# A one-core mixture-of-experts layer: the first expert pair's rows by a one-hot matmul, and the output stored from ScalarE's queue

## The chip, the cores and the metric

The kernel runs on one core of a Trainium2 chip. A core has TensorE (PE, with its weight load as PEld), VectorE (DVE), ScalarE (ACT), GpSimd (POOL) and SyncE (SP). Each works through its own row of instructions and waits at semaphores for the others. DMAs are issued from an engine's queue (SPq, ACTq, POOLq) and carried out by sixteen DMA engines. The metric is the device time in microseconds of one execution, and the times given are those of several runs.

## The reference

A decoder layer on 512 tokens of 1024 features. The front end (stick-breaking attention beside spatial gating, one input and one output projection) gives h. A router then picks one group of experts and two experts in it for each token:

```python
hn = rmsnorm(h, ffn_norm_g)
h  = h + hierarchical_moe(hn, ...)   # 4 groups of 8 experts, top 1 group, top 2 experts
out = rmsnorm(h, final_norm_g)
# one expert: silu(hn @ w_gate) * (hn @ w_up), times its weight, @ w_down; F = 512
```

All 32 experts have weights of their own: three matrices of 1024 x 512 in fp32, 201 MB in all.

## The kernel before, in words

The tokens lie in four chunks (c = 0 to 3) of 128 partitions, and h stays in SBUF. After the attention, the output projection is worked in eight units u (chunk and half), each followed at a distance by the router's steps. A string of letters for each unit sets their order: o and O are the projection's matmuls, A adds them to h, q squares, t transposes h (`turn`), l gives the logits `lg`, r and R go on with `route` (the small VectorE operations that end in `oab`, the two one-hot choices of each token), m and p give the position of each token in its expert's list (`pos_mm` on TensorE, `positions` on VectorE), M gathers the lists in PSUM (`rows_mm`). The last string, u = 8, is the tail after the last projection. Behind it comes chunk 3 by itself, in the order of the code.

`store_xn(c)` writes the normalized rows of a chunk to the DRAM tensor xn_d. Its ScalarE copy puts feature 8p+k at place (k, p), so that a row of 1024 splits into eight blocks of 128. The gate and up weights are loaded in the order that goes with it.

The experts work in 16 pairs (p = 0 to 15), 64 slots for each expert, so that a pair has 128 rows. `gather(xg, GI[:, p])` is an indirect DMA from GpSimd's queue that fetches the pair's 128 rows of xn_d; GI is made from the lists (`stl` and `gi` in the trace). `prep` transposes the rows in eight blocks on TensorE (`px`) and scales by the norm's gain into XS[p] (`xs`): four blocks on ScalarE, four in one VectorE operation. Then gate and up (`gu`, 32 matmuls for each expert), the activation (`sg`, `gg`, `hg`), down (`y`), the split of y in `yh` and `yl`, and the one-hot matmuls that add the rows back into h (`cb`, at the end `cl`). `busy(pool, tag, n)` makes TensorE work on products that nobody reads (`idle` in the trace). After the lists, VectorE works out counts (`cnt`, `tot`, `cop`, `okt`). The count `n_over` of rows that find no slot is read by four engines into a register (`values_load`, a TENSOR_LOAD), and `If` blocks on such counts jump over the overflow's work, which has nothing to do with these inputs except for the few rows of `xgo`.

The weights come in 192 loads of 1 MiB from SyncE's queue (`load_next`, L592 and L590) into 19 half slots that are freed by the matmuls which read them. The loads stand in SyncE's row in a fixed order, each with a wait for its slot. One small DMA stands among them: `mark_d` takes 16 numbers of the first gather's result to DRAM, and what follows it in SyncE's row comes after it.

The tail: for the last pair `down`, `results` (which makes `yh` and `yl`), then `unit(c, n)` adds half n of chunk c into h, `squares` and `scale_3` make the final norm's factor (GpSimd raises to the power), `gained` and `finish` multiply by gain and factor into fin, and `finish` stores the chunk from SyncE's queue (L1254). Last there is an `If(n_over > OVER)`, L1338, which all engines jump over.

## Time and profile before

| what | value |
|---|---|
| median of 3 runs | 750.05 us (746.28 to 752.68) |
| the profiled execution | 752.61 us |
| its span in the trace | 750.6 us |
| mean granted clock of TensorE | 0.966 |
| PE, DVE, ACT, POOL busy | 706.2, 303.8, 230.1, 81.0 us |
| DMA | 231.03 MB, 308 GB/s over the span |

The span runs from the first to the last instruction that the profiler saw; 2.0 us of the execution lie around it. A queue has a q behind its engine's name. PEclk is the clock that TensorE was granted, as a share of 2.4 GHz, and DMA share is how busy the sixteen DMA engines were in a window.

### The profile page before, as it was taken

The numbers are of one execution on the slowest core, as the hardware profiler recorded it, in microseconds if no ns is written. First come the engines' busy times: TensorE is split into PE (matmuls) and PEld (weight loads), VectorE is DVE, ScalarE is ACT, GpSimd is POOL, SyncE is SP. The second block draws the span as 40 slices with busy tenths as digits, with TensorE's granted clock in tenths as the row PEclk, the third lists the DMA queues.
The fourth block names the chain that finished last, engine by engine and source line by source line (L and its number), as shares of the span: only waits on it lengthen the run. The fifth ranks groups of instructions, "written<-read, shape, count | busy, mean of one in ns | idle before, by whom it ended". The sixth has DMA issues, their size and how long they took to land. (4 is left out here: it accounts for less than half of the span.)

```text
span 750.6 us, 9187 instructions
## 1 busy us (share of the span) xinstructions
PE 706.2 (94%) x3426; PEld 400.1 (53%) x3426; DVE 303.8 (40%) x540; ACT 230.1 (31%) x383; POOL 81.0 (11%) x77
## 2 busy tenths in 40 slices
PE   8999999999999799999999998999999999899992
PEld 7776767678788646444443443334344444344431
DVE  5547558375575712313422403033043133042345
ACT  5564568546345512111211211111111111121124
POOL 0322132114121201000000000000000000000001
PEclk9989699899999899999999999999999999999998
DMA  8802010206629789799999999999999999999953
GB/s 269 347 8 105 1 56 29 84 1 222 241 97 415 269 339 412 303 419 420 417 420 420 417 421 419 420 420 419 419 419 420 417 420 418 421 415 420 406 210 117
DMA packets 42392, 231.03 MB, mean 308 GB/s; under 512 B 6354, under 2 KB 8018, under 8 KB 18258
## 3 DMA queue, kind: packets, MB, share of 16 engines
q1 hardware_dynamic: 39394, 223.81, 73.7%
q0 software_dynamic: 2352, 4.20, 1.6%
q10 hardware_dynamic: 576, 2.10, 0.7%
q8 instruction: 43, 0.70, 0.4%
q14 instruction: 27, 0.22, 0.1%
HBM read 230.22 MB, written 4.19 MB: 312 GB/s over the span
## 5 line engine op out<-in xcount | busy, mean ns | idle before, releaser
L981 PE MATMUL gu<-r,xs 128*64 128x512 f32 x1024 | 229.5, 598 | 9.0 <-DMA r<-w_up 4.7
L981 PEld LDWEIGHTS gu<-r,xs 128*64 128x64 f32 x1024 | 86.2, 138 | 149.9 <-issue 131.6
L1011 PE MATMUL y<-r,hg 128*64 128x512 f32 x512 | 114.3, 596 | 0.0
L993 DVE TENSOR_TENSOR hg<-ft,gg 128x256 f32<-128x256 f32 x32 | 13.4, 420 | 228.5 <-ACT gg L991 221.4
L987 ACT COPY sg<-gu 128x512 f32<-128x512 f32 x32 | 18.7, 586 | 225.0 <-PE gu L981 225.0
L1045 DVE TENSOR_TENSOR h<-cb,h 128x512 f32<-128x512 f32 x120 | 74.2, 681 | 0.0
L1011 PEld LDWEIGHTS y<-r,hg 128*64 128x64 f32 x512 | 35.9, 136 | 66.3 <-issue 51.3
L914 POOL DMA_INDIRECT xg<-xn_d,gi x16 | 16.5, 1028 | 379.1 <-PE px L962 371.6
L1032 DVE SCALAR_TENSOR_TENSOR yl<-y,tab,yh 128x512 fp32r<-128x512 f32 x32 | 23.8, 750 | 66.8 <-ACT yh L1031 65.4
L1039 PE MATMUL cb<-yh,oh 128*128 128x512 f32 x120 | 49.9, 416 | 0.0
L1039 PE MATMUL cb<-yl,oh 128*128 128x512 f32 x120 | 47.3, 394 | 0.0
L1031 ACT ACTIVATE yh<-y,tab 128x512 fp32r<-128x512 f32 x32 | 21.8, 687 | 75.5 <-PE y L1011 74.6
L116 PE MATMUL pT<-xhi,hl_w 128*128 128x512 f32 x80 | 35.2, 440 | 0.0
L117 PE MATMUL pT<-xlo,hl_w 128*128 128x512 f32 x80 | 33.8, 423 | 0.0
L118 PE MATMUL pT<-xhi,hl_w 128*128 128x512 f32 x80 | 33.7, 421 | 0.0
L111 POOL TENSOR_TENSOR hl_w<-wqk,hl_w 128x1024 fp32r<-128x1024 f32 x10 | 24.3, 2434 | 69.5 <-ACT hl_w L110 67.2
L965 ACT ACTIVATE xs<-px,ffk 128x128 f32<-128x128 f32 x64 | 18.2, 368 | 32.5 <-PE px L962 32.5
L116 PE MATMUL pR<-hl_w,xhi 128*128 128x512 f32 x64 | 26.4, 413 | 0.0
L117 PE MATMUL pR<-hl_w,xhi 128*128 128x512 f32 x64 | 26.1, 407 | 0.0
L118 PE MATMUL pR<-hl_w,xlo 128*128 128x512 f32 x64 | 25.9, 405 | 0.0
L999 PEld LDWEIGHTS ft<-identf,sg 128*128 128x128 f32 x128 | 14.6, 140 | 21.1 <-issue 16.1
L1039 PEld LDWEIGHTS cb<-yh,oh 128*128 128x128 f32 x120 | 22.6, 188 | 4.5 <-DVE h L1045 0.2
(262 smaller groups left out, 939.0 us busy)
## 6 DMA issues: line engine op xcount, KB each, us to landing
r<-w_gate SPq DMA_DIRECT2D x64, 1024.0 KB, 19.9
r<-w_up SPq DMA_DIRECT2D x64, 1024.0 KB, 19.9
r<-w_down SPq DMA_DIRECT2D x64, 1024.0 KB, 20.3
wqk<-w_inT SPq DMA_DIRECT2D x10, 512.0 KB, 4.5
wr<-w_inR SPq DMA_DIRECT2D x8, 512.0 KB, 7.3
wo<-w_out SPq DMA_DIRECT2D x8, 512.0 KB, 4.6
xt<-xT SPq DMA_DIRECT2D x8, 256.0 KB, 5.3
h<-xr SPq DMA_DIRECT2D x4, 512.0 KB, 10.0
```

The costliest lines, as they stand in the source:

```text
L111: (nc.gpsimd if pool else nc.vector).tensor_tensor(lo, src, hi.bitcast(F32), op=OP.subtract)
L116: nc.tensor.matmul(ps, lh, rh, start=first, stop=False)
L117: nc.tensor.matmul(ps, lh, rl, start=False, stop=False)
L118: nc.tensor.matmul(ps, ll, rh, start=False, stop=last)
L965: nc.scalar.activation(xs[:, k], px[:, k, :xs.shape[2]], AF.Copy, scale=ffk[:, k:k + 1])
L981: nc.tensor.matmul(ps[rs_], xs[:, k], w, start=k == 0, stop=k == KD - 1, skip_group_check=True)
L987: nc.scalar.copy(SG[e], GU[e].rearrange("s (p j) -> s j p", j=4))
L1011: nc.tensor.matmul(YS[p][n][rs_], HT[e][:, j], down_weights(e, j, n), start=j == 0, stop=j == 3, skip_group_check=True)
L1031: nc.scalar.activation(yh[:, cs], YS[p][n], AF.Copy, scale=tab[:, 1, p:p + 1])
L1032: nc.vector.scalar_tensor_tensor(yl[:, cs], YS[p][n], tab[:, 1, p:p + 1], yh[:, cs].bitcast(F32), op0=OP.mult, op1=OP.subtract)
L1039: nc.tensor.matmul(ps, OHT[p][:, c * P:(c + 1) * P], y[:, n * 512:(n + 1) * 512], start=first and i == 0, stop=last and i == 1, skip_group ...
L1045: nc.vector.tensor_tensor(h[:, c, cs], ps, h[:, c, cs], op=OP.add)
```

## The change

The first pair's rows no longer go through DRAM. `first_slots(c)` makes a one-hot `own` for each chunk on VectorE (128 tokens by 128 slots, with the token's norm factor as its value): two operations for q, the slot numbers of the tokens that chose expert 0 or 1, and two comparisons with `slot1`. `first_rows(c, ...)` multiplies h by it on TensorE, eight 128x128 fp32 products for each chunk, summed over the chunks in the PSUM tiles pf0 and pf1. They hold what the transposes held before, and `with_gain` scales them into XS[0]. The letters S and V place `first_slots`, 1 and 2 place `first_rows` for chunk 0; chunks 1 and 2 come after `store_xn(3)`, chunk 3 after its `pos_mm` and `first_slots`. The gather of pair 1 is now the first gather, and stands where that of pair 0 stood. mark_d, all the `busy` calls shown and the load of a second gain vector go. `positions(1)` moves from u = 8 to u = 7. xn keeps the natural order of the features, and the host lays the gate and up weights out to suit; bytes and shapes of the loads stay.

In the tail, the last pair's down for its second half is done in one piece, ahead of the units, with `results(1)` right behind it and `places` after `results(0)`. The four stores are issued by ScalarE, and SyncE has nothing left ahead of the last branch.

The diff, with hunks of little content left out:

```diff
     "o s r R q t m p O A w l M a",
-    "o r R q t m p O A w l M a",
+    "o r R q t m p O A w l M S a",
     "o s r R q t m p O A w l M a",
-    "z q t m k p l M",
+    "z q 1 t 2 m k S p V l M",
 )
...
     xn_d = dram.tile([T, D], F32, name="xn_d")
-    mark_d = dram.tile([1, 16], F32, name="mark_d")
...
     dma(wrs, wr)
-    ffgs = rw.tile([P, KD], F32, name="ffgs")
-    dma(ffgs, ffg)
     brB = rw.tile([P, 36], F32, name="brB")
...
     ffk = keep.tile([P, KD], F32, name="ffk")
-    dma(ffk, ffp)
+    dma(ffk, ffg)
     load_next(2)
...
-        xn[c] = rw.tile([P, KD, P], F32, tag="xn", bufs=2, name=f"xn{c}")
-        nc.scalar.activation(xn[c], h[:, c].rearrange("t (p k) -> t k p", k=KD), AF.Copy, scale=rs2[:, c:c + 1])
+        xn[c] = rw.tile([P, D], F32, tag="xn", bufs=2, name=f"xn{c}")
+        nc.scalar.activation(xn[c], h[:, c], AF.Copy, scale=rs2[:, c:c + 1])
         nc.scalar.dma_start(xn_d[c * P:(c + 1) * P], xn[c])
+    own = rw.tile([P, NCH, P], F32, name="own")
+    slot1 = rw.tile([P, SLOTS], F32, name="slot1")
+    nc.gpsimd.iota(slot1, pattern=[[1, SLOTS]], base=1, channel_multiplier=0, allow_small_or_imprecise_dtypes=True)
+    px0 = []
+    def first_slots(c):
+        q = rw.tile([P, 2, 2], F32, tag="q", bufs=2, name=f"q{c}")
+        nc.vector.tensor_tensor(q[:, 0], oab[:, 0, c, :2], oab[:, 1, c, :2], op=OP.add)
+        nc.vector.scalar_tensor_tensor(q[:, 1], pos_ps[:, c * 32:c * 32 + 2], 1.0, q[:, 0], op0=OP.add, op1=OP.mult)
+        for r, rs_ in halves:
+            nc.vector.tensor_scalar(own[:, c, rs_], slot1, q[:, 1, r:r + 1], rs2[:, c:c + 1], op0=OP.is_equal,
+                                    op1=OP.mult)
+    def first_rows(c, *ks):
+        if not px0:
+            px0.extend(op_.tile([P, 4, P], F32, tag="o", name=f"pf{n}") for n in range(2))
+        for kk in ks:
+            nc.tensor.matmul(px0[kk // 4][:, kk % 4], h[:, c, kk * P:(kk + 1) * P], own[:, c],
+                             start=c == 0 and kk % 4 == 0, stop=c == NCH - 1 and kk % 4 == 3, skip_group_check=True)
...
             pos_mm(2 if u == 8 else (u - 5) // 2)
-        elif x == "p" and u in (5, 8):
-            for k in (0,) if u == 5 else (1, 2):
-                positions(k)
+        elif x == "p" and u in (5, 7, 8):
+            positions({5: 0, 7: 1, 8: 2}[u])
+        elif x in "SV":
+            first_slots({"S": u - 7 + (u == 6), "V": 2}[x])
+        elif x in "12":
+            first_rows(0, *((0, 1, 2) if x == "1" else (3, 4, 5, 6)))
         elif x == "w" and u == 0:
             for k in range(KD):
-                nc.vector.tensor_scalar(wrs[:, k], wrs[:, k], ffgs[:, k:k + 1], None, op0=OP.mult)
+                nc.vector.tensor_scalar(wrs[:, k], wrs[:, k], ffk[:, k:k + 1], None, op0=OP.mult)
         elif x == "l" and u > 0:
...
     store_xn(3)
+    first_rows(0, 7)
+    for c in (1, 2):
+        first_rows(c, *range(KD))
     go(16, R[3])
...
     nc.scalar.activation(ge, gd, AF.Exp)
-    busy(op_, "o", 2)
     nc.scalar.activation(rr, dd, AF.Exp)
-    busy(op_, "o", 2)
     nc.scalar.preload_act_table_set("silu_and_others")
     pos_mm(3)
+    first_slots(3)
     positions(3)
+    first_rows(3, *range(KD))
     rows_mm(sps, soh, (3,))
...
-    gather(xg, GI[:, :1])
-    dma(mark_d, xg[:1, :16])
+    gather(xg, GI[:, 1:2])
     load_next(1)
...
-    wp.close()
-    attp.close()
     rws.close()
...
     nc.gpsimd.memset(xgo, 0.0)
+    XS, GU, SG, HT, YS, YT, OHT = {}, {}, {}, {}, {}, {}, {}
+    def with_gain(xs, px, n):
+        if n == 0:
+            for k in range(4):
+                nc.scalar.activation(xs[:, k], px[:, k, :xs.shape[2]], AF.Copy, scale=ffk[:, k:k + 1])
+        else:
+            nc.vector.tensor_tensor(xs[:, 4:], px[:, :, :xs.shape[2]],
+                                    ffk[:, 4:, None].to_broadcast([P, 4, xs.shape[2]]), op=OP.mult)
+    XS[0] = mo.tile([P, KD, P], F32, tag="xs", name="xs0")
+    for n in range(2):
+        with_gain(XS[0], px0[n], n)
+    wp.close()
+    attp.close()
     psg = ctx.enter_context(tc.tile_pool(name="psg", bufs=2, space=PS))
...
     NP = E // 2
-    XS, GU, SG, HT, YS, YT, OHT = {}, {}, {}, {}, {}, {}, {}
...
         return psm.tile([P, *shape], F32, tag="m", name=name)
-    busy(psm, "m", 6)
...
                 nc.tensor.transpose(px[:, k], x[:, kk * P:(kk + 1) * P], identf)
-            if n == 0:
-                for k in range(4):
-                    nc.scalar.activation(xs[:, k], px[:, k, :xs.shape[2]], AF.Copy, scale=ffk[:, k:k + 1])
-            else:
-                nc.vector.tensor_tensor(xs[:, 4:], px[:, :, :xs.shape[2]],
-                                        ffk[:, 4:, None].to_broadcast([P, 4, xs.shape[2]]), op=OP.mult)
+            with_gain(xs, px, n)
...
     onehot(ohf, slotf, pos, SLOTS)
-    busy(psm, "m", 4)
-    prep_pair(0)
     zb = mo.tile([P, P], BF, name="zb")
...
             combine(p - 1, 6, 7)
-            places(p)
             down_over(p)
...
     clear(False)
-    yo2 = mo.tile([P, 2, 512], F32R, tag="xs", name="yo2")
+    yo2 = [mo.tile([P, 512], F32R, tag="xs", name="yo2a"), mo.tile([P, 512], F32R, tag="sg", bufs=2, name="yo2b")]
     for n, rs_ in halves:
-        nc.scalar.activation(yo2[:SLOTS, n], yo[rs_], AF.Copy, scale=tabo[rs_, 1:2])
-        nc.vector.scalar_tensor_tensor(yo2[SLOTS:, n], yo[rs_], tabo[rs_, 1:2], yo2[:SLOTS, n].bitcast(F32),
+        nc.scalar.activation(yo2[n][:SLOTS], yo[rs_], AF.Copy, scale=tabo[rs_, 1:2])
+        nc.vector.scalar_tensor_tensor(yo2[n][SLOTS:], yo[rs_], tabo[rs_, 1:2], yo2[n][:SLOTS].bitcast(F32),
                                        op0=OP.mult, op1=OP.subtract)
...
         add_rows(ps, p, 2 * c + n, True, False)
-        nc.tensor.matmul(ps, oho[:, c * P:(c + 1) * P], yo2[:, n], start=False, stop=True, skip_group_check=True)
+        nc.tensor.matmul(ps, oho[:, c * P:(c + 1) * P], yo2[n], start=False, stop=True, skip_group_check=True)
         into_h(ps, 2 * c + n)
...
-    def finish(c, queue):
+    def finish(c):
         sc = rs3[:, c:c + 1]
...
         nc.vector.scalar_tensor_tensor(fin[c][:, 512:], h[:, c, 512:], sc, finB[:, 512:], op0=OP.mult, op1=OP.mult)
-        queue.dma_start(out[c * P:(c + 1) * P], fin[c])
+    def store(c):
+        nc.scalar.dma_start(out[c * P:(c + 1) * P], fin[c])
...
     results(p, (0,))
-    down(p, (1,), (0, 1))
+    places(p)
+    down(p, (1,))
+    results(p, (1,))
     for c in range(NCH):
...
         squares(c, 0)
-    down(p, (1,), (2, 3))
     for c in range(NCH):
         gained(c)
-    results(p, (1,))
     for c in range(NCH):
...
             scale_3(c - 1)
+        if c == 3:
+            store(0)
         if c > 1:
-            finish(c - 2, nc.sync)
+            finish(c - 2)
     scale_3(3)
-    finish(2, nc.sync)
-    finish(3, nc.sync)
+    finish(2)
+    store(1)
+    finish(3)
+    store(2)
+    store(3)
...
         "w_out": c(w_out[0].reshape(2, NCH, P, D).transpose(0, 2, 1, 3)),
-        "ffp": c(ffn_norm_g[0].reshape(P, KD)),
         "ffg": cols(ffn_norm_g[0], KD),
...
         "br": c(br.reshape(1, 36)),
-        "w_gate": c(w_gate.reshape(E, P, KD * F)),
-        "w_up": c(w_up.reshape(E, P, KD * F)),
+        "w_gate": c(w_gate.reshape(E, KD, P, F).transpose(0, 2, 1, 3).reshape(E, P, KD * F)),
+        "w_up": c(w_up.reshape(E, KD, P, F).transpose(0, 2, 1, 3).reshape(E, P, KD * F)),
         "w_down": c(w_down.reshape(E, P, 4 * D)),
```

The first place is PE's row between the last lists and the first gate and up. Before, from the end of the totals over all experts (`pos_ps` with `onesb`):

```order
1008 L909 LDWEIGHTS onesb
1009 L909 MATMUL pos_ps<-oab,onesb 128x32
1010 L187 MATMUL idle<-identf 128x128 x10
1011 L962 MATMUL px_0_2135<-identf,xg 128x128 x4
1012 L962 MATMUL px_1_2144<-identf,xg 128x128 x4
1013 L1125 TENSOR_LOAD cnt
1014 L981 MATMUL gu_2172<-r_0_0_1208,xs_2134 64x512
```

Ten idle products, eight transposes and the read of the count lay between the totals and `gu`. After, from the lists of chunk 2 (`sps` with `soh`), from the positions of chunk 3, and from the end of the totals:

```order
971 L853 MATMUL sps<-code,soh 64x32
972 L758 MATMUL pf_1958<-own,h 128x128
973 L758 MATMUL pf_1957<-own,h 128x128 x4
974 L758 MATMUL pf_1958<-own,h 128x128 x4
975 L758 MATMUL pf_1957<-own,h 128x128 x4
976 L758 MATMUL pf_1958<-own,h 128x128 x4
...
993 L758 MATMUL pf_1957<-own,h 128x128 x4
994 L758 MATMUL pf_1958<-own,h 128x128 x4
995 L853 LDWEIGHTS soh
...
1018 L934 MATMUL pos_ps<-oab,onesb 128x32
1019 L1153 TENSOR_LOAD cnt
1020 L1011 MATMUL gu_2194<-r_0_0_1207,xs_2131 64x512
```

Seventeen `pf` products now stand between the lists of chunk 2 and the positions of chunk 3, and eight more between those and the lists of chunk 3; idle products and transposes are gone, and the read of the count follows the totals.

The second place is DVE's row from the counts to the operand of the first gate and up. Before:

```order
240 L933 SCALAR_TENSOR_TENSOR tot<-cop,tot 128x1
241 L934 TENSOR_SCALAR okt<-tot 128x1
242 L1103 CAST cnt<-tot 128x1
243 L1104 TENSOR_SCALAR cnt<-cov,okt 128x32
244 L1105 TENSOR_SCALAR cnt<-cop,okt 128x16
245 L726 TENSOR_REDUCE gst<-ge 128x4
...
253 L819 TENSOR_TENSOR ohf<-slotf,pos 128x512
254 L967 TENSOR_TENSOR xs_2134<-px_1_2144,ffk 128x512
255 L1125 TENSOR_LOAD cnt
```

Here `xs` stood behind the counts and the one-hot `ohf`. After:

```order
252 L957 SCALAR_TENSOR_TENSOR tot<-cop,tot 128x1
253 L958 TENSOR_SCALAR okt<-tot 128x1
254 L975 TENSOR_TENSOR xs_2131<-pf_1958,ffk 128x512
255 L1133 CAST cnt<-tot 128x1
256 L1134 TENSOR_SCALAR cnt<-cov,okt 128x32
257 L1135 TENSOR_SCALAR cnt<-cop,okt 128x16
258 L723 TENSOR_REDUCE gst<-ge 128x4
```

Now `xs` stands ahead of `cnt<-tot`, the number that PE's TENSOR_LOAD reads, and `ohf` comes later.

The third place is the end of the kernel, on ACT and SP. ACT before (`sq` are the squares, `fin` the finished rows):

```order
604 L1233 ACTIVATE sq,ms_6696<-h 128x512 x3
605 L1252 ACTIVATE fin_6686<-fin_6686,rs_6697 128x512
606 L1233 ACTIVATE sq,ms_6696<-h 128x512
607 L1252 ACTIVATE fin_6686<-fin_6686,rs_6697 128x512
608 L1252 ACTIVATE fin_6687<-fin_6687,rs_6697 128x512 x2
609 L1338 COMPARE_AND_BRANCH
```

There is no store in it. ACT after:

```order
604 L1260 ACTIVATE sq,ms_6717<-h 128x512 x7
605 L1279 ACTIVATE fin_6706<-fin_6706,rs_6718 128x512
606 L1260 ACTIVATE sq,ms_6717<-h 128x512
607 L1283 DMA res<-fin_6706 128x1024
608 L1279 ACTIVATE fin_6706<-fin_6706,rs_6718 128x512
609 L1279 ACTIVATE fin_6707<-fin_6707,rs_6718 128x512
610 L1283 DMA res<-fin_6706 128x1024
611 L1279 ACTIVATE fin_6707<-fin_6707,rs_6718 128x512
612 L1283 DMA res<-fin_6707 128x1024 x2
613 L1372 COMPARE_AND_BRANCH
```

The first store now stands behind the last `sq`, the second between the last two `fin`, the others behind them. SP before, with the four stores (`res`) ahead of its branch:

```order
261 L1220 DMA fin_6688<-fing 128x1024
262 L1146 UNCONDITIONAL_BRANCH
263 L1254 DMA res<-fin_6686 128x1024 x2
264 L1254 DMA res<-fin_6687 128x1024 x2
265 L1338 COMPARE_AND_BRANCH
```

SP waited here for each `fin`. SP after, from the last weight loads:

```order
257 L589 DMA r_3_1_6325<-w_down 128x4x512
258 L589 DMA r_3_1_6327<-w_down 128x4x512
259 L1247 DMA fin_6708<-fing 128x1024
260 L1174 UNCONDITIONAL_BRANCH
261 L1372 COMPARE_AND_BRANCH
```

The stores are gone from it, and the branch follows the load of the final gain and the jump over the last pair's `If`.

## Rows read from the trace of the kernel before

**Rows 1.** The page: busy time of each engine, its share and instructions.
```profile
PE 706.2 (94%) x3426; PEld 400.1 (53%) x3426; DVE 303.8 (40%) x540; ACT 230.1 (31%) x383; POOL 81.0 (11%) x77
```

**Rows 2.** Waits of PE, 610 to 700 us: in total, times, longest.
```profile
PE gu L981 <- DMA r<-w_up: 4.7, 4, 2.1
```

**Rows 3.** Two stretches by windows: engines busy, PEclk, DMA share, GB/s.
```profile
306.00:308.00 2.00, 1.69 (x12) 0.79 (x9) 0.00 (x0) 0.64 (x2) 0.00 (x0) 1.00 0.00 0
600.00:700.00 100.00, 93.42 (x430) 42.53 (x430) 30.43 (x53) 14.88 (x35) 2.97 (x3) 0.98 1.01 419
```

**Rows 4.** Waits of the queue of SP, whole span.
```profile
SPq L592 <- PEq L1187: 44.2, 6, 14.6
...
SPq L919 <- DMA xg<-xn_d,gi: 15.6, 1, 15.6
```

**Rows 5.** Timeline, first pair: start, us, engine, line, operation, tiles.
```profile
249.96 0.75 DVE L625 SCALAR_TENSOR_TENSOR h<-o,rb,h 128x512 f32<-128x512 f32 x1 [0.81 <-PE o L118]
...
253.35 0.26 DVE L768 SCALAR_TENSOR_TENSOR L<-lg,rs,brB 128x36 f32<-128x36 f32 x1 [0.24 <-PE lg L752]
...
256.74 0.24 DVE L785 TENSOR_SCALAR oab<-o_s,o_m 128x32 bf16<-128x32 f32 x1
...
258.61 0.17 DVE L841 SCALAR_TENSOR_TENSOR gi<-sps,stl 128x16 int32<-128x16 f32 x1
...
259.16 4.01 PE L187 MATMUL idle<-identf 128*128 128x128 f32 x20 [0.47 <-DVE cov L930]
...
259.63 0.14 DVE L1103 CAST cnt<-tot 128x1 int32<-128x1 f32 x1
259.67 1.28 POOL L914 DMA_INDIRECT xg<-xn_d,gi  x1 [7.26 <-DVE tot L933]
...
259.90 1.10 DVE L1105 TENSOR_SCALAR cnt<-cop,okt 128x16 int32<-128x16 f32 x1
...
264.03 1.09 PE L962 MATMUL px<-identf,xg 128*128 128x128 f32 x8 [0.85 <-DMA xg<-xn_d,gi]
...
265.16 0.69 DVE L967 TENSOR_TENSOR xs<-px,ffk 128x512 f32<-128x512 f32 x1 [2.12 <-PE px L962]
...
265.24 1.08 PE L981 MATMUL gu<-r,xs 128*64 128x512 f32 x4
```

**Rows 6.** Timeline of PE, 296 to 309 us: the fourth gate and up.
```profile
299.88 7.09 PE L981 MATMUL gu<-r,xs 128*64 128x512 f32 x32
```

**Rows 7.** Timeline of the queue of SP, 245 to 312 us.
```profile
264.40 0.36 SPq L592 DMA_DIRECT2D r<-w_up  x1
...
307.10 0.33 SPq L592 DMA_DIRECT2D r<-w_up  x1
```

**Rows 8.** Windows of 2 us in the first pair's preparation, as in Rows 3.
```profile
256.00:258.00 2.00, 0.18 (x1) 0.00 (x0) 1.69 (x11) 0.97 (x5) 0.00 (x0) 0.50 0.39 160
262.00:264.00 2.00, 1.18 (x9) 0.98 (x7) 1.04 (x4) 0.00 (x0) 0.00 (x0) 0.90 0.32 115
```

**Rows 9.** The tile xn: its four stores, issue to landing.
```profile
DMA to landing us min/median/max: 3.3/7.9/8.8
```

**Rows 10.** Timeline, last 20 us.
```profile
734.85 0.74 DVE L1032 SCALAR_TENSOR_TENSOR yl<-y,tab,yh 128x512 fp32r<-128x512 f32 x1
...
736.42 1.38 DVE L1045 TENSOR_TENSOR h<-cl,h 128x512 f32<-128x512 f32 x2 [0.82 <-PE cl L1243]
...
740.23 3.08 SPq L1254 DMA_DIRECT2D res<-fin  x4
...
740.94 1.93 ACT L1252 ACTIVATE fin<-fin,rs 128x512 f32<-128x512 f32 x3
```

**Rows 11.** A window of 2 us in the last stores, as in Rows 3.
```profile
744.00:746.00 2.00, 0.00 (x0) 0.00 (x0) 0.00 (x0) 0.00 (x0) 0.00 (x0) 0.50 1.01 397
```

**Rows 12.** The last branch, L1338: durations in ns, then first and last start.
```profile
L1338 SPq EVENT_SEMAPHORE  x9: 17/17/17, 748.3 to 748.9; - x9
...
L1338 SPq COMPARE_BRANCH  x1: 45/45/45, 743.4 to 743.4; - x1
```

More of the change, by code (lines that the diff above doesn't have):

```diff
@@ L71, in layer_kernel @@
 @with_exitstack
-def layer_kernel(ctx, tc, xr, xT, gT, w_inT, w_inR, sgg, wsT, bsp, sbg, sog, w_out, ffp, ffg, wr, br,
+def layer_kernel(ctx, tc, xr, xT, gT, w_inT, w_inR, sgg, wsT, bsp, sbg, sog, w_out, ffg, wr, br,
                  w_gate, w_up, w_down, fing, out, dbg=None):
@@ L1370, in layer_kernel @@
             gained(c)
-            finish(c, nc.scalar)
+            finish(c)
+            store(c)
     begin.close()
```

## The prediction

> **What bounds the kernel now.** I read the page first: PE is busy 94% of the span, the other engines 40% or less [rows 1]. That alone would say that a microsecond taken from PE is a microsecond gained, but a share over the whole span hides where PE waits. So next the waits of PE in the late pairs: between 610 and 700 us gate and up wait 4.7 us for the loads of their weights [rows 2], and there the DMA engines are full, at 419 GB/s [rows 3]. In the last third the stream of weights sets the time, and PE has some slack.
>
> That doesn't make an earlier first pair worthless, and the reason is one hole in the stream. From 306 to 308 us nothing is moved at all, with PE busy all the time [rows 3]. The queue of SP stands at PE's branch of the pairs' `If` for up to 14.6 us [rows 4] and issues its next load at 307.10 [rows 7], just after the fourth gate and up, which begins at 299.88 and lasts 7.09 to 306.97 [rows 6]. The slots free up by PE's progress, and between the first gate and up and this restart PE hardly pauses. The first gate and up begins at 265.24 [rows 5]; I call this T0. The restart is T0 + 41.86. From it to the last weights the DMA engines are full, so the end moves with T0, one for one, as long as the hole stays: the bound from below is nothing gained, if the hole closes. By the same hole, loads that come earlier than 264 us are worth nothing by themselves: they make the hole longer.
>
> So two places count: what T0 becomes, and the tail behind the last weights.
>
> **T0, what is removed.** The lists of the last chunk end with `gi` at 258.61 + 0.17 = 258.78. Then come the indirect DMA on GpSimd (issued at 259.67 in 1.28), its flight, the transposes at 264.03 and T0 at 265.24 [rows 5]: 6.46 us from `gi` to `gu`, all of which goes for pair 0. The ten idle products (4.01 us) lie inside the flight and cost nothing now.
>
> **T0, what is added.** Four steps, each in the path before `gu`.
>
> (1) Ahead of chunk 3's router. Three `pf` products stand between the logits and the transposes of u = 8, four more behind the transposes, and two `first_slots` with one `positions` in VectorE's row. The nearest row for a `pf` is the idle product of the same shape and type: 20 rows for ten products, 4.01 us, so 0.40 each [rows 5], at half clock (the windows from 256 us show 0.50 [rows 8]), and about 0.20 at full; I use 0.22. Four `first_slots` operations are small, like `oab` (0.24, and the next starts 0.2 later); about 0.7 for the four. `h` of the last half now starts at 249.96 and takes 0.75 [rows 5]; with 0.7 more ahead of it on VectorE, which had 0.81 of idle there, it is 0 to 0.7 later, and the four `pf` add 0.9 on PE, partly beside ScalarE's copy. L was at 253.35. Bounds are 0 and 2.2 (seven products and the 0.7); I take 1.35, in the middle, because PE had gaps there to take some. `oab` then ends at 256.98 + 1.35 = 258.3.
>
> (2) Chunks 1 and 2. Seventeen `pf` take 3.8 us at full clock from about 254.6, so they end at 258.4, as `oab` does. Hidden, but with nothing to spare; at half clock they would take 6.8 and be 3 us late. I expect full clock: before, the fall to half followed a stretch in which PE worked little (0.18 of 2.00 us from 256 to 258 [rows 8]), and this stretch is now filled.
>
> (3) Chunk 3. Positions on PE (0.3), `first_slots(3)` (0.75), eight `pf` (1.8 at full clock, 3.2 at half), lists (0.3), `stl` and `gi` (0.5): 3.6, against 1.8 before. `gi` ends at 258.3 + 3.6 = 261.9, that is 3.1 later than before. VectorE's `positions(3)` runs beside the `pf`.
>
> (4) From `gi` to `gu`. Now the counts come into the path, which lay under the gather: `cnt<-tot` stood at 259.63 + 0.14 [rows 5], 1.0 after `gi`, and PE reads the number before gate and up. `xs` (0.69 [rows 5]) is now ahead of it. So 261.9 + 1.0 + 0.7 = 263.6, and the count is written at 263.7. Register read and branch on PE up to the first matmul: at least 0.1 (the transposes end at 264.03 + 1.09 = 265.12, and `gu` starts at 265.24), at most 1.3, the longest small step here [rows 5]; I take 1.0, since a write of another engine has to be seen first. T0 = 264.7.
>
> There is a catch at this place. The gather of pair 1 is issued on GpSimd 0.9 after `gi`, just when `xs` and `cnt<-tot` are due. In the trace a small VectorE operation that ran beside the gather took 1.10 us, `cnt<-cop` at 259.90, where its neighbours take 0.2 [rows 5]. If the count is caught, T0 is later by up to 0.9, and nothing of the gain is left. It needs the two to meet within a microsecond, so I take 0.2 of it: T0 = 264.9, 0.3 us earlier than before. The Trainium skill has a rule here (SBUF — State Buffer, "SBUF: two separate sides"): VectorE and GpSimd share a pair of ports under an exclusive lock, and the loser is blocked for the whole instruction. By it the count would wait for the whole gather instruction, and the sum would be T0 = 265.6, later than before; the stretched row agrees with it, and whether the two meet is not to be read from before.
>
> The other edits have one answer each: the contiguous ScalarE copy is faster than the strided one but ends ahead of its need; mark_d's removal lets the next load go up to 15.6 us [rows 4] earlier than at 264.40 [rows 7], which the hole takes up; the order of the weights' features changes no bytes; the lost gain load was 4 KB. One of them can cost: with a megabyte in the queue ahead of it the store of xn's chunk 3 may land late (3.3 to 8.8 us [rows 9]), and `xs` on ScalarE and the second gather wait for it. Between 0 and 1.5.
>
> **The tail.** `results(1)` now comes ahead of the units, so `yl` of the second half, at 734.85 before [rows 10], is done first, and its 0.74 are moved ahead of the first `h` and gained back where VectorE then goes straight on. The `h` of the second half started at 736.42, after 0.82 of idle [rows 10]; by VectorE's row it would start at about 736.9. Then ScalarE: its three `fin` start at 740.94 and take 1.93 [rows 10], and two store issues of about 0.4 now stand among them. The last store was issued at 740.23 + 3.08 = 743.3 at the end of SP's row [rows 10]; with 0.5 from VectorE and 0.8 from ScalarE it is 744.4, 1.1 later. The stores fill the DMA engines, 1.01 from 744 to 746 [rows 11], so two megabytes take 5.3 us at 397 GB/s from the first issue, and landing slips less than issue: 0.5 to 1.6, I take 1.2. The Trainium skill (DMA: Bandwidth & Descriptors, "Issuing engines are not separate DMA queues") says that another issuing engine saves only the sequencer's issue time. By it the move buys the stores nothing.
>
> What it buys is SP. SP took the last branch at 743.4 and began the semaphores behind it at 748.3 [rows 12]: 4.9 us, in which the stores landed too: from 740.23, with 1.5 to the first bytes (an estimate from the windows' rise) and 5.3, at about 747.0. Now it is there in good time and waits for the stores. With landing at 748.2 it goes on at 748.2 instead of 748.3. So the tail gives 0.1; were the stores not late it would give 1.3, and at the slow end of their landing it costs 0.8.
>
> **The sum.** T0 gives 0.3, the tail 0.1, the late xn store nothing (its lower end): 0.4. Profiled 752.61 becomes 752.2, with the span 750.2 and the same 2.0 around it. The median shown is 750.05, 2.6 lower than the profiled execution, so 749.6 there.
>
> **The rivals.**
> (a) *The gather is simply gone.* If the router's step isn't delayed and the counts stay hidden, `gi` still ends near 260.3 and `gu` follows in 1.2: T0 = 261.5, 3.7 earlier, with the tail's 1.3 that is 5.0: 745.0 from the median. For it speaks the 6.46 us from `gi` to `gu`; against it, eight products on PE and three VectorE steps in the path, whatever the rest does. 0.18.
> (b) *Slower: PE falls to half clock in `pf`.* The gate decides it: before, PEclk was 0.50 from 256 us and 0.90 only from 262 us [rows 8]. If the row between 254 and 258 us has pauses, seventeen products end at 261 instead of 258.4 and the eight at 0.40 each take 3.2: T0 up to 266.9, 1.6 later; with the tail's 0.1 off that 1.5: 751.55. It decides once the seventeen end later than `oab` does. Less likely, as PE has a long row without waits there. 0.15.
> (c) *The change doesn't do what it says in the tail*: SP's early branch helps (1.3 gained), while T0 stays: 748.75. 0.15.
> (d) *A transfer that is hidden anyway:* if the last weights don't move with T0, because the hole is filled by the earlier loads, T0 is worth nothing either way and only the tail counts: 749.95, hardly to be told from the forecast. 0.12.
> The forecast itself has 0.40.
>
> **How the numbers follow.** Predicted 749.6, that of the likeliest case. Its own range is 747.9 to 751.3 (T0 by 0.9 either way, the tail by 0.8). The range over the cases goes from (a), 745.0, to (b) with a late xn store, 751.55 + 1.0 = 752.5. A measurement of this kernel tells about 1%, 7.5 us, from no change. No case passes it: the best is 5.0, the worst 2.5. What is left for either side is what no row shows, 0.05 for faster and 0.04 for slower.
>
> **What would show it.** Right: `gu` starts within a microsecond of 264.9, `gi` ends near 262, PEclk stays at 1.00 from 254 to 262, `cnt<-tot` stands between `xs` and the first `gu`, the DMA hole ends 41.9 after `gu` starts, SP's branch stands far ahead of the stores and its semaphores follow the last landing at once, and the last store is issued about 1 us later, counted from the last down matmul. Wrong: a `gu` before 263, or a restart of the stream that doesn't follow T0, or `pf` products that wait for the one-hot.

## The result and the profile after

| | before | after |
|---|---|---|
| median | 750.36 us (746.28 to 752.82, 20 runs) | 753.72 us (748.97 to 758.20, 20 runs) |
| ratio, 95% interval | | 1.0053 (1.003 to 1.0076) |
| profiled execution | 752.61 us | 754.44 us |
| its span | 750.6 us | 752.6 us |

The changed kernel is slower by 0.5%: 3.4 us between the medians, 2.3 to 5.7 by the interval. Forecast were 0.4 us less and a range up to 752.5. So the sign was wrong, and the time lies above the range.

The two profiles can't be laid on each other as they stand, because the front end, which the change doesn't touch, took a different time in each execution. Here is the first h of the output projection's eight units before, and then after (timeline of DVE):

```profile
221.54 0.75 DVE L625 SCALAR_TENSOR_TENSOR h<-o,rb,h 128x512 f32<-128x512 f32 x1 [1.24 <-PE o L118]
```

```profile
219.76 0.75 DVE L624 SCALAR_TENSOR_TENSOR h<-o,rb,h 128x512 f32<-128x512 f32 x1 [1.24 <-PE o L117]
```

The changed kernel's timeline at the first pair:

```profile
248.59 0.74 DVE L624 SCALAR_TENSOR_TENSOR h<-o,rb,h 128x512 f32<-128x512 f32 x1
...
253.42 0.25 DVE L787 SCALAR_TENSOR_TENSOR L<-lg,rs,brB 128x36 f32<-128x36 f32 x1
...
258.16 2.05 PE L758 MATMUL pf<-own,h 128*128 128x128 f32 x16 [0.89 <-DVE own L750]
...
260.31 0.37 PE L934 MATMUL pos_ps<-oab,onesb 128*128 128x32 bf16 x8
...
260.63 0.17 DVE L860 SCALAR_TENSOR_TENSOR gi<-sps,stl 128x16 int32<-128x16 f32 x1
...
261.69 1.28 POOL L939 DMA_INDIRECT xg<-xn_d,gi  x1 [10.67 <-ACT xs L973]
261.75 0.69 DVE L975 TENSOR_TENSOR xs<-pf,ffk 128x512 f32<-128x512 f32 x1
262.36 0.14 DVE L1133 CAST cnt<-tot 128x1 int32<-128x1 f32 x1
262.42 1.70 DVE L1134 TENSOR_SCALAR cnt<-cov,okt 128x32 int32<-128x32 f32 x1
...
262.98 0.96 POOL L966 MEMSET xgo<- 128x1024 f32 x1
...
263.60 8.78 PE L1011 MATMUL gu<-r,xs 128*64 128x512 f32 x32 [2.92 <-issue]
```

The first h came at 221.54 before and at 219.76 after, 1.78 us apart with next to nothing changed ahead of it. In the profiles of this case it lies between 215.6 and 221.5. I therefore count the front from the start of this h, called H, and the tail from the end of the last gate and up, called G.

From H, the last L (the router's logits) came 31.81 before (253.35) and 33.66 after (253.42): 1.85 later. The gate and up of the first pair came 43.70 before (265.24) and 43.84 after: the 6.46 us of the gather's path are gone, and nothing is gained. But the row that decides is the last one: this first gate and up took 8.78 us, where it took 7.09 before, and it stands behind 2.92 us in which PE had nothing to do. The lines above it show why: the totals (`pos_ps` with `onesb`) end at 260.68, the operand `xs` and then the count are written by VectorE up to 262.50, and only then can PE read the number. The windows show the clock around the pause (columns as in Rows 3, PEclk third from the right):

```profile
258.00:260.00 2.00, 1.84 (x16) 1.84 (x16) 0.70 (x6) 1.07 (x1) 0.00 (x0) 1.00 0.07 27
260.00:262.00 2.00, 0.68 (x14) 0.43 (x13) 1.39 (x9) 1.03 (x4) 0.31 (x1) 1.00 0.11 16
262.00:264.00 2.00, 0.40 (x2) 0.23 (x4) 2.00 (x5) 0.11 (x1) 1.99 (x3) 1.00 0.89 262
264.00:266.00 2.00, 2.00 (x8) 0.78 (x6) 1.88 (x11) 0.00 (x0) 0.36 (x2) 0.56 0.94 379
266.00:268.00 2.00, 2.00 (x8) 0.71 (x6) 0.35 (x2) 0.00 (x0) 0.00 (x0) 0.59 0.07 27
```

From 260 to 264 PE was busy 0.68 and 0.40 of 2.00 us, still at full clock, and from 264 to 268 us the granted clock was 0.56 and 0.59, that is, mostly the lower level of 1.2 GHz, inside the first gate and up (263.60 to 272.38). The loads on SP's queue follow PE:

```profile
248.22 0.33 SPq L591 DMA_DIRECT2D r<-w_up  x1
261.00 0.33 SPq L591 DMA_DIRECT2D r<-w_gate  x1
...
307.22 0.33 SPq L591 DMA_DIRECT2D r<-w_up  x1
```

Two loads now go before 262 us, where `mark_d` held them until 264.40 [rows 7]. It was of no use: the stream restarted at 307.22, which is H + 87.46, against H + 85.56 before (307.10 [rows 7]). The restart came 43.6 behind the start of the first gate and up instead of 41.86, and nearly all of the difference is the 1.69 by which that gate and up was longer.

The rest is in the tail. The last gate and up ends at 720.62 before and 720.57 after, but the span ends 30.0 behind it before and 32.0 after. The timeline of the tail:

```profile
731.30 0.75 DVE L1062 SCALAR_TENSOR_TENSOR yl<-y,tab,yh 128x512 fp32r<-128x512 f32 x1 [2.09 <-ACT yh L1061]
...
736.77 1.28 DVE L1075 TENSOR_TENSOR h<-cl,h 128x512 f32<-128x512 f32 x2
...
739.87 0.68 DVE L1075 TENSOR_TENSOR h<-cl,h 128x512 f32<-128x512 f32 x1
...
740.95 0.63 ACT L1260 ACTIVATE sq<-h 128x512 f32<-128x512 f32 x1 [0.41 <-DVE ms L1264]
741.05 2.06 ACTq L1283 DMA_DIRECT2D res<-fin  x1
...
743.16 1.33 ACT L1279 ACTIVATE fin<-fin,rs 128x512 f32<-128x512 f32 x2 [1.49 <-POOL rs L1265]
...
744.52 1.27 ACTq L1283 DMA_DIRECT2D res<-fin  x2
```

The issue of the first store held ScalarE's queue for 2.06 us, where SP's took about 0.35. The next `fin` waited behind it, at 743.16, though the last square had ended at 741.58, and the last store was issued 24.56 behind G, against 22.30 (742.92) before. The DMA view of 741 to 743 us holds one single packet, and that is code (40 slices of 0.05 us):

```profile
DMA  0000000000040000000000000000000000000000
...
q14 instruction: 1, 0.01, 1.1%
```

The last branch, L1338 before and L1372 after:

```profile
L1372 SPq EVENT_SEMAPHORE  x9: 17/17/17, 720.6 to 750.9; - x9
...
L1372 SPq COMPARE_BRANCH  x1: 45/45/45, 715.2 to 715.2; - x1
```

SP came to it at 715.2, as intended, 28 us earlier than before. It still finished 2.0 us later (its last semaphore at 750.9, against 748.9 in [rows 12]), because it waits for the last landing. Its longest wait there ended at 750.4 (720.6 and 29.8; waits of SP's queue: in total, times, longest):

```profile
SPq L1372 <- SPq L1372: 35.2, 2, 29.8
```

Before, the stores ended between 747.4 and 747.8:

```profile
747.40:747.80 0.40, 0.00 (x0) 0.00 (x0) 0.00 (x0) 0.00 (x0) 0.00 (x0) 0.50 0.06 20
747.80:748.20 0.40, 0.00 (x0) 0.00 (x0) 0.00 (x0) 0.00 (x0) 0.00 (x0) 0.50 0.00 0
```

After, between 749.6 and 750.0:

```profile
749.60:750.00 0.40, 0.00 (x0) 0.00 (x0) 0.00 (x0) 0.00 (x0) 0.00 (x0) 0.50 0.05 20
750.00:750.40 0.40, 0.00 (x0) 0.00 (x0) 0.00 (x0) 0.00 (x0) 0.00 (x0) 0.50 0.00 0
```

Most of what these windows moved is a code packet; the stores' last packet was at 747.45 before and at 749.65 after. SP went on 0.85 us behind it before, when its branch was late (748.3 [rows 12]), and 0.75 behind it after, when it was early. So all but 0.1 or 0.2 of the 4.9 us of the late branch lay under the stores.

### The profile page after: what moved, and what is told of

Read it like the earlier page. It is cut to its first block, busy times and chain, and to the rows that moved or that the text cites. A ratio compares the mean times of both kernels' runs of the same rounds, so it can differ in the third digit from the quotient of the medians.

```text
span 752.6 us, 9252 instructions
## 1 busy us (share of the span) xinstructions
PE 702.6 (93%) x3454; PEld 399.1 (53%) x3454; DVE 308.3 (41%) x556; ACT 226.0 (30%) x383; POOL 80.5 (11%) x77
## 5 line engine op out<-in xcount | busy, mean ns | idle before, releaser
L115 PE MATMUL pR<-hl_w,xhi 128*128 128x512 f32 x64 | 25.4, 396 | 0.0
L116 PE MATMUL pR<-hl_w,xhi 128*128 128x512 f32 x64 | 25.1, 392 | 0.2 <-DVE hl_w L110 0.2
```

The source lines that it names most:

```text
L115: nc.tensor.matmul(ps, lh, rh, start=first, stop=False)
L116: nc.tensor.matmul(ps, lh, rl, start=False, stop=False)
```

## The experiments

The theory at the outset: 1.9 of the loss is TensorE's clock at the first gate and up, which the idle products had held up, and 2.0 is the tail, where ScalarE's first store is held; from the second group of experiments on (e5) the theory for that hold was that ScalarE waits for its own code. The rival was that the one or the other part is innocent, and inside the tail, that the order of the work or an idle queue is to blame and not the code. All times of the table are from the one profiled execution of each kernel, in us; the ratio is that of the timed runs. The restart is the first load of weights behind the hole in the stream.

| kernel | gate and up 1 from H | its length | restart from H | last store from G | end from G | ratio to before (95%) |
|---|---|---|---|---|---|---|
| before | 43.70 | 7.09 | 85.56 | 22.30 | 30.0 | 1 |
| after | 43.84 | 8.78 | 87.46 | 24.56 | 32.0 | 1.0053 (1.003 to 1.0076) |
| e1 front only | 43.81 | 8.62 | 87.28 | 22.34 | 29.8 | 1.0013 (0.9985 to 1.0042) |
| e2 tail only | 44.27 | 7.09 | 86.13 | 24.74 | 32.0 | 1.0021 (0.9989 to 1.0053) |
| e3 idle products back | 43.96 | 7.09 | 85.89 | 24.57 | 31.9 | 1.0019 (0.9991 to 1.0047) |
| e4 count first | 43.00 | 7.09 | 84.93 | 22.34 | 30.0 | 0.9972 (0.9947 to 0.9998) |
| e5 24 in the jumped block | 43.81 | 10.05 | 88.71 | 22.70 | 30.1 | 1.0005 (0.9978 to 1.0031) |
| e6 early small DMA | 43.82 | 7.09 | 85.76 | 23.50 | 30.8 | 1.0031 (0.9999 to 1.0064) |
| e7 stores from SP | 43.83 | 8.61 | 87.28 | 23.26 | 30.6 | 1.0037 (1.0007 to 1.0068) |
| e8 before, no idle products | 44.14 | 8.51 | 87.43 | 22.30 | 29.7 | 1.0015 (0.9989 to 1.0041) |
| e9 repaired | 43.01 | 7.09 | 84.93 | 22.69 | 30.1 | 0.9993 (0.9964 to 1.0021) |
| e10 6 in the jumped block | 43.82 | 8.54 | 87.19 | 23.18 | 30.6 | one run only |
| e11 = e4 | 43.02 | 7.09 | 84.94 | 22.32 | 30.1 | 1.0003 (0.9974 to 1.0033) |

Between restart and G all thirteen lie at 413.5 with 0.7 to either side, so the two landmarks hold all that differs. The sum of restart from H, 413.5 and end from G is 529.1 before and 533.0 after: 3.9 us, inside the interval of the measured ratio. The ratios of the single experiments can mostly not be told from no change: a difference of one or two microseconds is smaller than what the front end varies by. What follows rests on the traces.

**e1, the front alone** (the tail's part of the diff taken back).

> The front part of the change alone, with the old tail. Theory (the loss in front is TensorE's clock: with the idle products gone PE waits about 2.9 us for the count, its granted clock falls to half a microsecond into the first gate and up, and that takes 8.8 instead of 7.1 us): first gate and up 8.6 to 8.9 us, first load behind the hole in the stream about 1.9 us later against the first h of the output projection than before, 1 to 2 us slower than before. Rival (the whole loss is in the tail): same time as before or up to 0.5 us faster.

The restart came 1.72 later than before and the tail was as before. The theory's numbers came in the trace, and there the rival falls: the front loses by itself. The timed ratio, 1.0013, can't tell the two apart.

**e2, the tail alone** (the front's part taken back).

> The tail part alone, with the old front. Theory (the stores from ScalarE's queue are late, the first issue holds the queue 2 us): 1.5 to 2.5 us slower than before, the last store issued about 2.5 us later behind the last down than before, an issue of about 2 us among the four. Rival (the loss is in front only): same time as before or up to 1.3 us faster, all four issues 0.3 to 0.4 us.

The end came 2.0 later behind G, with one issue of 2.23 us among the four. The front part is not needed for it.

**e3, idle products put back** behind the totals of the changed kernel:

```diff
+    busy(op_, "o", 9)
     GI = rows(sps)
```

> The changed kernel with nine idle products put back between the totals and the read of the count. Theory (clock): the first gate and up again 7.1 us, begins 0 to 0.4 us later than without them, the stream restarts 1.3 to 1.7 us earlier, the run is that much faster than the changed kernel, 1.5 to 2.5 slower than before because of the tail. Rival (idle products are free, the loss is elsewhere): first gate and up at 8.8 us, no gain.

```profile
261.55 2.25 PE L186 MATMUL idle<-identf 128*128 128x128 f32 x18
264.74 7.09 PE L1012 MATMUL gu<-r,xs 128*64 128x512 f32 x32 [0.94 <-PE idle L186]
```

In PE's timeline nine products (18 rows) stand in the pause, and gate and up took 7.09 us again, with a start only 0.12 later. The restart came 1.57 earlier than in the changed kernel.

**e8, the idle products taken from the kernel before**, and nothing else:

```diff
-    busy(op_, "o", 2)
-    busy(psm, "m", 6)
-    busy(psm, "m", 4)
```

> The kernel before without its idle products around the first pair, nothing else changed. Theory (clock): the first gate and up starts 0 to 0.3 us earlier but takes 8 us or more instead of 7.09, so the stream restarts 1 to 2 us later against the first h of the output projection (86.5 to 87.5 instead of 85.56). Rival (they cost nothing to leave out): 7.09 and 85.3 to 85.6.

```profile
263.48 1.94 PE L959 MATMUL px<-identf,xg 128*128 128x128 f32 x8 [5.13 <-DMA xg<-xn_d,gi]
265.34 8.51 PE L978 MATMUL gu<-r,xs 128*64 128x512 f32 x32
```

Its windows, PEclk third from the right:

```profile
262.00:264.00 2.00, 0.52 (x3) 0.56 (x4) 0.69 (x2) 0.00 (x0) 0.00 (x0) 0.50 0.20 74
...
266.00:268.00 2.00, 2.00 (x8) 0.51 (x6) 0.60 (x2) 0.00 (x0) 1.19 (x3) 0.50 0.99 414
```

The same loss without any of the change: the transposes took 1.94 instead of 1.09 [rows 5], gate and up 8.51, and the restart came 1.87 later. Only the start was missed a little: 0.44 later, because the transposes were slow too. e3 and e8 together show it from both sides: taking the products out costs about what putting them in gives back. But the clock went another way in the two kernels. In the kernel before it was low already, 0.50 from 256 to 258 us, and 0.90 from 262 to 264 [rows 8], behind the first idle products; without them it was still 0.50 from 266 to 268. So there the idle products brought the clock back up, while in the changed kernel it was at 1.00 ahead of the pause, and e3's products kept it there.

**e6 and e5 bear on the clock as well**, by accident, since their front is that of the changed kernel. With the same pause and the same start, e6 kept full clock (its windows):

```profile
258.00:260.00 2.00, 0.00 (x0) 0.00 (x0) 1.84 (x10) 1.14 (x4) 1.28 (x1) 1.00 0.51 82
260.00:262.00 2.00, 1.40 (x8) 0.66 (x10) 1.88 (x8) 0.00 (x0) 1.39 (x3) 1.00 0.97 401
262.00:264.00 2.00, 2.00 (x12) 0.78 (x10) 1.38 (x6) 0.00 (x0) 0.00 (x0) 1.00 0.52 201
```

PEclk stayed at 1.00 and gate and up took 7.09, while e5's took 10.05. So the pause doesn't bring the fall each time: of six profiles with the front of the change and no idle products in it, five fell (8.54 to 10.05), and one didn't. Of the six profiles with idle products there (before, e2, e3, e4, e9, e11), all took 7.09. What decides between them is not known from these runs.

**e4, the count first.** The old tail, idle products in the pause, and the count of `n_over` ahead of `xs`:

```diff
+    busy(op_, "o", 6)
     GI = rows(sps)
 ...
     nc.vector.scalar_tensor_tensor(tot, cop[:, :1], float(OVER), tot, op0=OP.mult, op1=OP.add)
+    nc.vector.tensor_copy(cnt[:, 32:33], tot)
     nc.vector.tensor_scalar(okt, tot, float(OVER), None, op0=OP.is_le)
 ...
-    nc.vector.tensor_copy(cnt[:, 32:33], tot)
```

> The front part with the old tail, six idle products behind the totals, and the count of rows without a slot written right behind its sum, ahead of the operand of gate and up. Theory: the first gate and up begins about 1 us earlier than in the changed kernel and takes 7.1 us, so the end is 0.5 to 1.2 us earlier than before. Rival (the stream restarts by something else than PE's progress): same time as before.

```profile
257.76 0.15 DVE L959 CAST cnt<-tot 128x1 int32<-128x1 f32 x1
...
257.96 0.69 DVE L977 TENSOR_TENSOR xs<-pf,ffk 128x512 f32<-128x512 f32 x1
258.57 1.76 DVE L1135 TENSOR_SCALAR cnt<-cov,okt 128x32 int32<-128x32 f32 x1
...
258.97 1.51 PE L1013 MATMUL gu<-r,xs 128*64 128x512 f32 x6 [0.65 <-ACT xs L975]
```

`cnt<-tot` is done at 257.91 now, just as the gather of the next pair begins on GpSimd (257.90), and gate and up starts 1.06 behind it, as it started 1.10 behind the count in the changed kernel (262.50 to 263.60). `xs` is done by then (258.65): what starts gate and up is still the read of the count. From the totals' end to gate and up it is 2.1 us instead of 2.9. The restart lies at 84.93, 0.63 before that of the kernel before. The timed ratio was 0.9972 here and 1.0003 when the same kernel ran again (e11, below), so the gain of 0.6 us is in the traces and not in the times.

**e7, the stores from SP** in the changed order:

```diff
-        nc.scalar.dma_start(out[c * P:(c + 1) * P], fin[c])
+        nc.sync.dma_start(out[c * P:(c + 1) * P], fin[c])
```

> The changed kernel with the four stores issued from SyncE, in the changed order of the tail. Theory A and B alike (the loss of the tail is the ScalarE issue): the last store is issued 22.3 to 22.9 us behind the last gate and up, the end 29.7 to 30.5 behind it, 1.5 to 2.3 us earlier than the changed kernel. Rival (the new order of down and results costs it): issue at 24 and more.

No issue above 0.36 us, and the end 1.4 earlier than in the changed kernel. But the last store at 23.26 is 0.4 later than I had expected, and 0.96 later than before. So part of the tail's loss isn't the issue. ScalarE's last square started 0.41 behind VectorE's h instead of 0.10, as in the changed kernel (739.87 + 0.68 = 740.55 to 740.95), and e5 shows where this comes from.

**e5, code moved on ScalarE.** 24 operations in the last overflow block, which is jumped over:

```diff
+            if p == NP - 1:
+                for _ in range(24):
+                    nc.scalar.activation(padt, tabo[:, :1], AF.Copy)
```

> The changed kernel with 24 tiny ScalarE operations in the last overflow block, which is jumped over: they do nothing, but move ScalarE's code behind them by 24 instructions. Theory A (the 2 us at the first store are a wait for ScalarE's code, at a fixed place of it): no store issue above 0.8 us, the last store is issued 1.2 to 1.8 us earlier behind the last gate and up (22.8 to 23.4 instead of 24.56), the end follows by 1 to 1.8. Theory B (the first DMA of a queue that has long been idle takes 2 us): the first issue again about 2 us, no change.

```profile
739.40 0.63 ACT L1265 ACTIVATE sq<-h 128x512 f32<-128x512 f32 x1
739.50 0.39 ACTq L1288 DMA_DIRECT2D res<-fin  x1
```

The issue took 0.39 us and the last store came at 22.70. The code packet, which came amid the stalled issue before, now came 8 us earlier behind G, among ScalarE's first squares, which took their usual 0.63 us each (DMA view of 731.5 to 733.5, 40 slices; two packets, of which the changed kernel has one at the same distance from G):

```profile
DMA  0000000000040000000500000000000000000000
...
q14 instruction: 2, 0.02, 2.5%
```

The late square of e7 and of the changed kernel is gone here too: it starts 20.08 behind G (739.40), where it was 20.38 (740.95), and against the changed kernel nothing else is different than where the code lies. So the order of the tail costs no more than the 0.4 that stay. They are VectorE's: the h of the second half starts 16.20 behind G here and in the changed kernel (736.77), where it started 15.80 behind it before (736.42 [rows 10]).

**e6, a small DMA ahead**, against the idle queue:

```diff
+    nc.scalar.dma_start(warm_d, tabo[:1, :16])
     ms3 = mo.tile([P, NCH, 2], F32, name="ms3")
```

> The changed kernel with a DMA of 64 bytes from ScalarE's queue some 15 us ahead of the first store. Theory A (code): that DMA is issued in 0.3 to 0.4 us, and the wait of some 2 us stays at the first store or at the instruction or two ahead of it. Theory B (idle queue): that DMA takes about 2 us, and the first store 0.3 to 0.4.

```profile
720.85 0.48 ACTq L1256 DMA_DIRECT2D warm_d<-tabo  x1
...
736.49 1.30 ACTq L1285 DMA_DIRECT2D res<-fin  x1
```

The small DMA was issued in 0.48 us, after some 470 us without any on that queue, and the first store, 16 us later, still took 1.30. An idle queue is not the cause. That it took 1.30 and not 2.06 fits the code, which this DMA moves too: the code packet came at 736.25 here, ahead of the issue, and the issue ended at 737.79, 1.5 behind it. This was not tested by itself.

**e10, six instead of 24.**

> As e5, with 6 operations in place of 24. If the wait is for ScalarE's code at a fixed place, it comes some 6 instructions earlier: ahead of the last square or at the first finished row, so that a gap of 1 to 2 us stands there and the first store is issued in 0.3 to 0.8 us. If the padding only changed something else (the queue, the timing of the stores), the first store takes about 2 us again, or there is no gap at all.

```profile
736.73 0.63 ACT L1265 ACTIVATE sq<-h 128x512 f32<-128x512 f32 x1
736.83 0.97 ACTq L1288 DMA_DIRECT2D res<-fin  x1
```

The gap did not move to another instruction, as I had expected of the theory. The first store still was the one that waited, but only 0.97 us. In the changed kernel the code packet came half a microsecond behind the start of the issue (741.55 to 741.60 in the view above, 741.05). Here it came ahead of it, at 736.25 to 736.30 with the issue at 736.83 (DMA view of 735 to 737):

```profile
DMA  0000000000000000000000000400000000000000
```

In both the issue ended some 1.5 us behind the packet, at 743.11 and at 737.80. Six instructions moved the packet by 1.4 us, from 21.0 to 19.6 behind G. That is what a fetch would do that is asked for at a fixed place of ScalarE's code, with the store as the first to need what it brings. In e2 and e3, with 2.23 and 2.05, the packet stands at 736.90 and 740.75, and the issue ended 1.7 and 1.5 behind it. e5 and e10, which change no executed operation, and e6 leave little room for a cause in the queue or in the stores themselves. Whose code a packet brings is not in the profile, so the wait for ScalarE's code is inferred from what moves with it.

**e9, the change repaired** with the edits of e4 and e5, its own tail kept.

> The whole change, repaired at three places: six idle products behind the totals, the count written right behind its sum, and the 24 ScalarE operations that are jumped over. Theory: first gate and up 43.0 us behind the first h of the output projection and 7.1 long, the stream restarts near 84.9, the end 30.1 behind the last gate and up as in e5; in all 0.3 to 0.8 us faster than before and about as fast as e4. Rival (the early branch of SyncE is worth its 4.9 us when the stores are in time): end at 28.7 behind the last gate and up.

The front came as in e4 and the end 30.1 behind G: both as expected, and the rival falls. SP's early branch gains nothing to be seen here, even with stores that are not held. By its landmarks the kernel is no faster than e11:

> The kernel of e4 once more, beside e9 on the same chip: faster than before by 0.5 to 1 us (0.1%), the stream restarts near 84.9 behind the first h, the end 29.8 to 30.0 behind the last gate and up.

The landmarks of e4 came again within 0.1 us; by them it is 0.5 us ahead of the kernel before, which the times (1.0003) can't confirm.

## Why the prediction was wrong

**The step that failed first** is the sentence that the ten idle products "lie inside the flight and cost nothing now". They were taken for what filled the gather's wait, and with the wait gone their removal was free. But in the kernel before they also brought the clock back for gate and up (e8). And in the changed kernel a wait was left, 2.9 us for the count, and nothing filled it. I had priced that wait as time (step 4: about 1.0 + 0.7 + 1.0 from `gi` to `gu`; 2.8 was measured, 260.80 to 263.60), but not as a pause of PE. The clock was in the prediction, as rival (b), in the wrong place: the `pf` products ran at full clock, as forecast, and the half clock came in gate and up, for 1.7 us, where (b) had 1.6.

**T0.** The single terms were near. L came 1.85 later, against 1.35: 0.41 of that came ahead of u = 8, where I counted nothing, and 1.44 in it. From L to gate and up it was 10.18 us, against 10.2 forecast (264.9 less 254.7). So a gain of 0.3 became a loss of 0.14, a mis-sized term. The catch did not come for the count: `xs` and `cnt<-tot` both started inside the gather's instruction (261.69 to 262.97) and took 0.69 and 0.14, as before. It came for the operation right behind them: `cnt<-cov` took 1.70 us, where it took 0.24 before (at 259.75). The rule of the Trainium skill that was quoted (SBUF — State Buffer, "SBUF: two separate sides") holds, on VectorE's side, for an operation in a 2-port mode or one with two SBUF inputs. The prediction left this condition out when it had the count wait, and the trace doesn't say which operations meet it. By the rule `cnt<-cov` would be blocked until the gather's instruction ends, 262.97. The trace shows longer: `cnt<-cov` ended at 264.12, after the memset that followed on GpSimd, at 263.94, which the rule allows only if that took the ports next.

**The stream.** That the end moves with PE's progress, and that loads which come earlier are worth nothing, held in all thirteen profiles (413.5 from restart to G). Only T0 was the wrong landmark: it is the end of the first gate and up that counts, and its length was taken as given. Rival (d) falls with it.

**The tail.** Forecast was a gain of 0.1, measured a loss of 2.0. "It is there in good time" was right for SP. The term that failed is ScalarE's: two issues at 0.4 each were 2.06 and 0.34, most likely because ScalarE waited for code (e5, e6, e10). No row of before showed this, and I bounded the issue by SP's rows alone. With the code moved (e5) the last store was 0.4 later than before, where 1.1 was forecast: VectorE's 0.5 came as 0.4, ScalarE's 0.8 didn't come. The sum itself was off: 743.3 with 0.5 and 0.8 is 744.6, and 743.3 is the end of the last issue, which began at 742.92. And the gain set against it, up to 1.3, was too high: I had put the last landing at 747.0, while the stores' last packet was at 747.45, and SP goes on some 0.75 us behind that packet even when it is early. The slow end of 0.8 does not follow from the landing's slip either: 747.0 with 1.6 is 748.6, 0.3 behind 748.3. The rule on the issuing engines (DMA: Bandwidth & Descriptors, "Issuing engines are not separate DMA queues" of the Trainium skill) was the better guide: it promised the stores nothing. What the runs add is that the new queue can cost something, by what else its engine does.

**The signs.** PEclk stayed at 1.00 ahead of `gu`, as the forecast wanted it, and `cnt<-tot` stood between `xs` and `gu`. But the hole ended 43.6 behind the start of `gu` instead of 41.9, and one sign of being wrong came: the last eight `pf` products waited 0.89 us for the one-hot (the row at 258.16).

**The chances.** The forecast had 0.91 for no change beyond 1%, and that is what happened. The range failed at its upper end: (b) had 1.6 for the front, near the 1.9 that came, but the worst that any case had for the tail was 0.8, and that case was not added to (b).

## What to carry to other kernels

Before idle work is removed from TensorE, look for every wait that is left in its row up to the next long stretch of matmuls, and price it twice: as time, and as a pause after which that stretch may start at half clock. When instructions are moved to another engine's row near the end of a kernel, look in the trace for the code packets as well as for the data: a fetch that is hidden in one layout can fall on the critical instruction in the next. And an instruction that comes too late costs only what it adds to a wait that is there anyway, here 0.1 or 0.2 of 4.9 us.

## What the hardware showed that was not expected

A store issue on ScalarE's queue took 2.06 us with a code packet amid it, 0.97 with the code moved by 6 instructions, and 0.39 with 24, without a change of one executed operation. A pause of 2.9 us on TensorE was followed by a granted clock of 0.56 to 0.59 in the next 4 us in one execution, and by 1.00 in another of the same front part. And a small VectorE operation that met the gather took 1.70 us, past the end of the gather's own instruction, while two others that started inside it, just ahead of this one, took no longer than before.
